# Values three units behind their scores, a fourth tile of transposed exponentials, and 2-D biases loaded by halves

## The chip, the cores and the metric

The kernel runs on one core of a Trainium2 chip. TensorE (PE in the profile) multiplies matrices into eight PSUM banks, VectorE (DVE), ScalarE (ACT) and GpSimd (POOL) work on tiles, and nearly all transfers are issued from SyncE's queue (SP). Each engine takes its instructions in order. The metric is the device time of one execution in microseconds (us); lower is better.

## The reference, cut to what matters

One encoder layer is computed for a prompt of 512 tokens and a sample of 1024 tokens, 1024 wide, with shared weights:

```python
h = rmsnorm(x);  q/k/v of heads A and B, gate logits = split(h @ w_in)
oa = neighborhood_attention(qa, ka, va, rpb)      # 8 heads, 8 x 16 windows on rows of 64 tokens, learned 2-D bias
ob = combine of dilated_group_attention(...)      # 3 groups (dilation 1, 4, 16) x 4 heads, T5 bias,
                                                  # weighted by each group's softmax denominator
x = x + (sigmoid(ga) * (oa @ w_a) + sigmoid(gb) * (ob @ w_b)) @ w_out
x = x + relu(rmsnorm(x) @ w_up)**2 @ w_down
```

All tensors are float32 outside; the kernel computes each product as three float16 matmuls of high and low halves.

## The kernel before, in words

**Stages.** Up to about 157 us the inputs are normalised, the first gate columns are multiplied and bias tables are built in device memory (tb_d, tc_d for B, ba_d for A). Then comes the attention stage, to about 985 us. After it the branch products, the output product and the MLP (dn and up in the profile) run to the end.

**Attention.** Heads are handled in ten pairs, i = 0 to 9: 0 to 5 are B (group g = i mod 3), 6 to 9 are A. ORDER (L39) sets their order, and each is done for the prompt (r = 0) and then for the sample (r = 1). A pair's work is cut into units of 128 queries: four for the prompt, eight for the sample, 120 in all. In the profile's names the first digit is r and the letter the kind: pT1a is the transposed exponentials of a sample A pair.

A unit has two parts. Its scores part (`scores`, L447 to L482) issues four matmuls into two PSUM banks, adds the bias and takes the minimum on VectorE (L462), exponentiates on ScalarE (L464), splits into two float16 halves (ScalarE L478, VectorE L479) in tile p16, and has SP transpose p16 by DMA into a tile of tag pT (L481). Its values part (`values`, L484 to L496) multiplies pT with the values from a tile of tag V (L492, L493), and evicts with ScalarE (L495) and VectorE (L496). An A unit is then normalised on POOL (L537) and stored to o_d by SP (L540); a B unit is stored with its minimum and denominator to g_d (L614).

**Order of the work.** Three generators are advanced in turn, one step each (`run`, L696 to L702). `attention` (L665 to L684) gives out a unit's scores in one step and may give out an older unit's values in the next, so a unit takes two steps. Values are given out when more than `lag` = NPT - 1 units stand in its queue, or when the oldest is AGE steps old; NPT is 3 and AGE 5 (L35, L36). `proj` (L348 to L444) gives in each step half of a 128-token projection (12 matmuls, pj in the profile), squares and normalises q and k, has SP transpose them into tiles qk0 (prompt) or qk1 (sample) (L389), and copies them on ScalarE and VectorE (L394, L395) some tiles later. After the pairs 6, 7 and 8 it gives six gate steps of 24 matmuls (g) each, and at its end the filler `fill`, five gates of three blocks. `combines` (L686 to L694) waits until a pair of group 2 has given out its last unit (`done`), lets eight steps pass, and then loads the three groups' outputs for 256 tokens into a tile G (L626), twice for the prompt and four times for the sample, weights them on VectorE, ScalarE and POOL (L633 to L653) and stores them to o_d (L654).

Within this program order the framework sets each engine's final order at build time, by its own estimate of when an instruction's inputs and buffers are ready.

**Tiles.** Those of one tag share a fixed number of buffers: pT has NPT = 3, V has NV = 5, bias 2, oB (a B unit's output) 4, oA 3, qk0 2, G 2, and mn, den and rd (an A unit's minimum, denominator and its reciprocal) 4 each. A pair's sample bias for A is a tile of 128 x 2 x 768 floats (768 KB, L544, L545) for the columns (0,), (1, 2) and (3,) of j; it serves two or four units. The blocks of x wait in tiles of the attention pool's tags before that stage: block 2's chunks 0 to 5 in two bias tiles (L775 to L777). The row of squared gains (L785) uses a G buffer.

Of the kernel before, what the change touches and what calls it, by code (L numbers as in the profile page):

```python
# [10 lines left out]
F32 = mybir.dt.float32  # L11
# [6 lines left out]
P = 128  # L18
D = 1024
# [12 lines left out]
VEC = 512  # L32
RPW = 63

NPT = 3  # L35
AGE = 5  # L36
NV = 5

ORDER = (0, 1, 2, 6, 3, 7, 4, 8, 5, 9)  # L39
# [91 lines left out]
def encoder(ctx, tc, xt, x, wg, wp, wb, wo, wu, wn, wd, nv, nvr, nmlp, nq, rpb, t5, oneh, negrow, cmask, yp, ys):  # L131
    nc = tc.nc
# [18 lines left out]
    ba_d = [drp.tile([HA, 16, 8, 1024], F32, name=f"ba_d{i}") for i in range(3)]  # L151
# [177 lines left out]
    class Attention:  # L329
# [172 lines left out]
        def attn_a(self, p):  # L502
            for _ in tab:
                pass
            pp, n = self.pp, p["name"]
            h0 = 2 * (p["i"] - 6)

            groups = ((0, 0, 8, 0),) if p["r"] == 0 else ((0, 0, 12, 0), (1, 4, 12, 384))
            c0, cn = (0, 256) if p["r"] == 0 else (256, 768)
            nrb = p["n"] // 256  # L510
            vsrc = self.va(p).rearrange("(r w) b d -> r w b d", w=GW)

            def load_v(j):
                v = self.vtile(f"{n}_{j}")
                nc.sync.dma_start(out=v[:, :nrb], in_=vsrc[:, A_K0[j]:A_K0[j] + 32])
                return v

            def make(j, bias, v, grp):
                blk, r0, nr, b0 = grp
                nm = f"{n}_{j}_{blk}"  # L520
                widths = [P] * (nr // 4)
                st = {}

                def s():
                    mn = pp.tile([P, 2], F32, tag="mn", bufs=4, name=f"mn{nm}")
                    den = pp.tile([P, 2], F32, tag="den", bufs=4, name=f"den{nm}")
                    st["p"] = self.scores(
                        nm, p, lambda q: q[:, (4 * blk + j) * P:(4 * blk + j + 1) * P],
                        lambda k: k.rearrange("p (r c) -> p r c", c=GW)[:, r0:r0 + nr, A_K0[j]:A_K0[j] + 32], widths,
                        [bias[:, h, b0:b0 + nr * 32] for h in range(2)], mn, den)  # L530
                    st["rd"] = pp.tile([P, 2], F32, tag="rd", bufs=4, name=f"rd{nm}")
                    nc.vector.reciprocal(out=st["rd"], in_=den)

                def v_():
                    ot = pp.tile([P, P], F32, tag="oA", bufs=3, name=f"o{nm}")
                    self.values(nm, p, st["p"], widths, [v[:, r0 // 4 + i] for i in range(nr // 4)], ot)
                    nc.gpsimd.tensor_tensor(out=heads(ot), in0=heads(ot), in1=bcast(st["rd"], HD), op=ALU.mult)  # L537
                    a = p["t0"] + blk * 512
                    dst = o_d[a:a + 512].rearrange("(r w) d -> w r d", w=GW)
                    nc.sync.dma_start(out=dst[16 * j:16 * j + 16, :, h0 * HD:h0 * HD + P], in_=ot)  # L540
                return s, v_

            for cg, js in enumerate(((0,), (1, 2), (3,))):
                bias = pp.tile([P, 2, cn], F32, tag="bias", bufs=2, name=f"ba{n}_{cg}")  # L544
                nc.sync.dma_start(out=bias, in_=ba_d[cg][h0:h0 + 2, :, :, c0:c0 + cn].rearrange("h c r k -> (c r) h k"))  # L545
                vt = [load_v(j) for j in js]
                for j, v in zip(js, vt):
                    for grp in groups:
                        yield make(j, bias, v, grp)


        def attn_b(self, p):
            pp, n, g, jj = self.pp, p["name"], p["g"], p["jj"]
            t0, L, nt = p["t0"], p["n"], p["nt"]
            gd = g_d[jj][t0:t0 + L, g]
            vd = v_d[p["i"]][t0:t0 + L]
            tiles = []
            if g < 2:
                bt = pp.tile([P, 2, 384], F32, tag="bias", bufs=2, name=f"b{n}")
                nc.sync.dma_start(out=bt, in_=tb_d[g][2 * jj:2 * jj + 2].rearrange("h p k -> p h k"))  # L560
            else:
                bt = pp.tile([P, 2, P], F32, tag="bias", bufs=2, name=f"b{n}")
                nc.sync.dma_start(out=bt, in_=tc_d[p["r"]][2 * jj:2 * jj + 2].rearrange("h p k -> p h k"))
            if g == 0:
                vts = [self.vtile(f"{n}_{i}") for i in range(-(-(nt + 1) // 4))]

                def chunk(c):
                    return vts[c // 4][:, c % 4, :]
                nc.sync.dma_start(out=chunk(0)[0:64], in_=vd[0:64])
                for i in range(len(vts)):  # L570
                    a, e = max(1, 4 * i), min(nt, 4 * i + 4)
                    if e > a:
                        nc.sync.dma_start(out=vts[i][:, a - 4 * i:e - 4 * i, :],
                                          in_=vd[64 + (a - 1) * P:64 + (e - 1) * P].rearrange("(c p) d -> p c d", p=P))
                nc.sync.dma_start(out=chunk(nt)[0:64], in_=vd[L - 64:L])
                for i in range(nt):
                    w = [64 if i == 0 else P, 64 if i == nt - 1 else P]
                    tiles.append((slice(i * P, (i + 1) * P), slice(max(0, i * P - 64), max(0, i * P - 64) + sum(w)), w,
                                  128 if i == 0 else 64, [chunk(i), chunk(i + 1)],
                                  gd[i * P:(i + 1) * P]))  # L580
            elif g == 1:
                vs = [self.vtile(f"{n}_{i}") for i in range(nt // 4)]
                for i, v in enumerate(vs):
                    nc.sync.dma_start(out=v, in_=vd[i * 512:(i + 1) * 512].rearrange("(i c) d -> i c d", c=4))
                m = nt // 4
                for c in range(4):
                    for i in range(m):
                        a = c + 4 * i * P
                        tiles.append((slice(a, a + 4 * P - 3, 4), slice(c, c + 4 * m * P - 3, 4), [P] * m, 128 - 128 * i,
                                      [v[:, c, :] for v in vs],  # L590
                                      gd.rearrange("(i c) d -> c i d", c=4)[c, i * P:(i + 1) * P]))
            else:

                vs = [self.vtile(f"{n}_{i}") for i in range(nt // 4)]
                for i, v in enumerate(vs):
                    nc.sync.dma_start(out=v, in_=vd.rearrange("(m c) d -> m c d", c=nt)[:, 4 * i:4 * i + 4])
                for t in range(nt):
                    a = slice(t, t + nt * (P - 1) + 1, nt)
                    tiles.append((a, a, [P], 0, [vs[t // 4][:, t % 4, :]], gd.rearrange("(m c) d -> c m d", c=nt)[t]))

            def make(ti):
                qs, ks, widths, boff, vch, dst = tiles[ti]
                nm = f"{n}_{ti}"
                w = sum(widths)
                st = {}

                def s():
                    o = st["o"] = pp.tile([P, 132], F32, tag="oB", bufs=4, name=f"o{nm}")
                    st["p"] = self.scores(nm, p, lambda q: q[:, qs], lambda k: k[:, ks], widths,
                                          [bt[:, h, boff:boff + w] for h in range(2)], o[:, 128:130], o[:, 130:132])  # L610

                def v_():
                    self.values(nm, p, st["p"], widths, vch, st["o"][:, :P])
                    nc.sync.dma_start(out=dst, in_=st["o"])  # L614
                return s, v_

            for ti in range(nt):
                yield make(ti)
            p["done"] = True
# [147 lines left out]
    with tc.tile_pool(name="attention", bufs=1, reuse_waits="tile") as pp:  # L767
        def load_x(b):

            if b < 2:  # L770
                x6 = pp.tile([P, 6, 512], F32, tag="qk1", bufs=2, name=f"xt{b}")
                xch[b] = [x6[:, k] for k in range(6)]
            else:
                xch[b] = []
                for i in range(2):  # L775
                    x3 = pp.tile([P, 3, 512], F32, tag="bias", bufs=2, name=f"xt{b}_{i}")
                    xch[b] += [x3[:, k] for k in range(3)]  # L777
            xch[b] += [pp.tile([P, 512], F32, tag="V", bufs=NV, name=f"xt{b}_{k}") for k in (6, 7)]
            for k, c in enumerate(xch[b]):
                xch["last"] = nc.sync.dma_start(out=c, in_=xt[b, :, k, :]).ins  # L780
                yield

        def gain():

            row = pp.tile([1, D], F32, tag="G", bufs=2, name="nvrow")  # L785
            nc.scalar.dma_start(out=row, in_=nvr)
            nc.vector.tensor_tensor(out=row, in0=row, in1=row, op=ALU.mult)
            mx = pp.tile([1, 2], F32, name="nvmax")
# [497 lines left out]
```

## Time and profile before

| what | before |
|---|---|
| median of 3 runs (lowest, highest) | 2255.98 us (2255.64, 2256.01) |
| the profiled execution, its time | 2257.27 us |
| its span, first to last instruction | 2255.5 us |
| TensorE, matmuls | 2131.3 us busy (94%), x11440 |
| TensorE, weight loads | 1085.5 us (48%) |
| VectorE | 1258.3 us (56%) |
| ScalarE | 1010.4 us (45%) |
| POOL | 314.6 us (14%) |
| mean granted TensorE clock | 0.985 |
| DMA, mean over the span | 111 GB/s |

The busy shares are averages over stages. In the MLP, more than half of the span, TensorE is busy throughout and its wait is for itself; what the change does must be read in the attention stage. A granted clock of 1.00 is 2.4 GHz, 0.5 is 1.2 GHz. "Idle before" an instruction is the time that its engine stood still ahead of it, and the releaser is what ended it.

### The profile page before, as it was taken

Reading aid. Unit: us, or ns where it says so; the run is one execution under the profiler, and the core shown is the slowest. Engines: PE = TensorE matmul, PEld = TensorE weight load, DVE = VectorE, ACT = ScalarE, POOL = GpSimd, SP = SyncE. Lnnn points to the kernel's source line nnn. Section 1 sums busy time; section 2 is a strip of 40 time slices with the busy share of each in tenths; the row PEclk is TensorE's granted clock in tenths of the full one; section 3 lists DMA queues with packets and bytes.
Section 4 is the critical chain, followed back from the end, with each engine's and each line's share of the span. In section 5 each row is a group of like instructions: output and inputs, shape, how many; then the busy total and the mean of one; then the engine's idle time right before and its main releaser. Section 6 shows DMA issues by size and latency. Waiting matters only on the chain.

```text
span 2255.5 us, 32279 instructions
## 1 busy us (share of the span) xinstructions
PE 2131.3 (94%) x11440; PEld 1085.5 (48%) x11440; DVE 1258.3 (56%) x3231; ACT 1010.4 (45%) x2435; POOL 314.6 (14%) x445
## 2 busy tenths in 40 slices
PE   5898899899989989899999999999999999999999
PEld 3355555455555555344444544444444444444444
DVE  7646767676577577556644644444444444444444
ACT  6346765477566566346622532222333333323222
POOL 5123332242232232100000000000000000000000
PEclk9899999999999999899999999999999999999999
DMA  6676656877776776877530111101111111110102
GB/s 202 203 237 144 140 133 143 171 167 163 160 165 132 158 153 135 191 238 237 159 108 29 57 56 49 35 30 57 57 57 56 56 57 56 56 37 24 34 1 112
DMA packets 342187, 251.23 MB, mean 111 GB/s; under 512 B 210432, under 2 KB 302464, under 8 KB 342024
## 3 DMA queue, kind: packets, MB, share of 16 engines
q1 hardware_dynamic: 341878, 249.15, 42.3%
q8 instruction: 90, 1.47, 0.3%
q14 instruction: 73, 0.60, 0.1%
q10 hardware_dynamic: 146, 0.01, 0.0%
HBM read 164.02 MB, written 53.29 MB: 96 GB/s over the span
## 4 chain that ended last, share of the span: by engine, by line
PE 54%; DMA 1%; issue 1%; ACT 0%; DVE 0%; SPq 0%; POOL 0%; ACTq 0%; DVEq 0%; POOLq 0%
PE up L174 7%; PE dn L174 7%; PE dn L176 7%; PE up L176 7%; PE up L175 7%; PE dn L175 7%; PE op L174 2%; PE op L176 2%; PE op L175 2%; PE br L174 1%; PE br L175 1%; PE br L176 1%; DMA z<-z_d 0%; DMA st_b<-in_wb 0%; PE hT L1041 0%
## 5 line engine op out<-in xcount | busy, mean ns | idle before, releaser
L943 DVE SCALAR_TENSOR_TENSOR y<-dn,und,y 128x512 f32<-128x512 f32 x384 | 287.1, 750 | 179.4 <-PE dn L176 178.8
L1121 ACT ACTIVATE r<-up,alpha 128x512 f32<-128x512 f32 x96 | 65.3, 681 | 592.1 <-PE up L176 592.0
L174 PE MATMUL up<-xp,w_u 128*128 128x512 f16 x768 | 291.0, 379 | 1.0 <-ACT xp L1044 1.0
L176 PE MATMUL dn<-w_d,u 128*128 128x512 f16 x768 | 291.1, 379 | 0.0
L176 PE MATMUL up<-xp,w_u 128*128 128x512 f16 x768 | 291.0, 379 | 0.0
L175 PE MATMUL dn<-w_d,u 128*128 128x512 f16 x768 | 291.0, 379 | 0.0
L175 PE MATMUL up<-xp,w_u 128*128 128x512 f16 x768 | 291.0, 379 | 0.0
L174 PE MATMUL dn<-w_d,u 128*128 128x512 f16 x768 | 291.0, 379 | 0.0
L1125 DVE TENSOR_TENSOR u<-r,u 128x512 f16<-128x512 f32 x96 | 66.4, 692 | 284.5 <-ACT u L1124 280.7
L174 PE MATMUL g<-act,w_g 128*128 128x512 f16 x384 | 148.6, 391 | 23.6 <-ACT act L802 13.7
L175 PE MATMUL g<-act,w_g 128*128 128x512 f16 x384 | 149.3, 389 | 7.4 <-DVE act L803 7.4
L176 PE MATMUL g<-act,w_g 128*128 128x512 f16 x384 | 149.4, 389 | 1.2 <-DVE w_g L263 1.0
L174 PE MATMUL pj1b<-w_p,act 128*128 128x384 f16 x384 | 126.1, 328 | 5.6 <-DVE qn0b L380 3.6
L175 PEld LDWEIGHTS <-act 128*128 128x128 f16 x960 | 96.2, 100 | 68.0 <-issue 15.6
L176 PEld LDWEIGHTS <-act 128*128 128x128 f16 x960 | 95.6, 100 | 65.7 <-issue 5.7
L174 PEld LDWEIGHTS <-act 128*128 128x128 f16 x960 | 96.8, 101 | 62.5 <-issue 4.8
L176 PE MATMUL pj1b<-w_p,act 128*128 128x384 f16 x384 | 125.9, 328 | 0.0
L175 PE MATMUL pj1b<-w_p,act 128*128 128x384 f16 x384 | 125.8, 328 | 0.0
L174 PEld LDWEIGHTS <-u 128*128 128x128 f16 x768 | 76.3, 99 | 88.9
L174 PEld LDWEIGHTS <-w_u 128*128 128x128 f16 x768 | 76.4, 100 | 88.5
L176 PEld LDWEIGHTS <-u 128*128 128x128 f16 x768 | 75.1, 98 | 90.7
L176 PEld LDWEIGHTS <-w_u 128*128 128x128 f16 x768 | 75.1, 98 | 90.5
(331 smaller groups left out, 4260.1 us busy)
## 6 DMA issues: line engine op xcount, KB each, us to landing
st_n<-in_wn SPq DMA_DIRECT2D x32, 512.0 KB
st_u<-in_wu SPq DMA_DIRECT2D x32, 512.0 KB
st_d<-in_wd SPq DMA_DIRECT2D x32, 512.0 KB
st_p<-in_wp SPq DMA_DIRECT2D x80, 192.0 KB
z_d<-z SPq DMA_DIRECT2D x48, 256.0 KB
z<-z_d SPq DMA_DIRECT2D x48, 256.0 KB
ba1a<-ba_d SPq DMA_DIRECT2D x12, 768.0 KB
xt<-in_xt SPq DMA_DIRECT2D x24, 256.0 KB
```

The source lines that it names most:

```text
L174: nc.tensor.matmul(ps, ah, bh, start=first, stop=False)
L175: nc.tensor.matmul(ps, ah, bl, start=False, stop=False)
L176: nc.tensor.matmul(ps, al, bh, start=False, stop=last)
L943: nc.vector.scalar_tensor_tensor(out=out, in0=ps, scalar=scale, in1=out, op0=ALU.mult, op1=ALU.add)
L1121: nc.scalar.activation(s, ps[b], AF.Relu, scale=alpha[:, f:f + 1])
L1125: nc.vector.tensor_tensor(out=uu[:, 1, i, tb], in0=s, in1=uu[:, 0, i, tb], op=ALU.subtract)
```

## The change

Values follow their scores by three units instead of two (lag = NPT - 1), or after 7 steps instead of 5, and there are four pT and five oB buffers. A's bias for the sample is loaded in two tiles of 384 columns, one for each block of 512 tokens, into three bias buffers; the units of columns 1 and 2 then run by block first (j 1, 2 of block 0, then of block 1). Block 2 of x uses one qk0 tile for three chunks and three bias tiles for three, and the gains' row uses a qk0 buffer.

```diff
-NPT = 3
-AGE = 5
+NPT = 4
+AGE = 7
...
-            groups = ((0, 0, 8, 0),) if p["r"] == 0 else ((0, 0, 12, 0), (1, 4, 12, 384))
-            c0, cn = (0, 256) if p["r"] == 0 else (256, 768)
+            groups = ((0, 0, 8, 0),) if p["r"] == 0 else ((0, 0, 12, 256), (1, 4, 12, 640))
...
-                        [bias[:, h, b0:b0 + nr * 32] for h in range(2)], mn, den)
+                        [bias[:, h] for h in range(2)], mn, den)
...
             for cg, js in enumerate(((0,), (1, 2), (3,))):
-                bias = pp.tile([P, 2, cn], F32, tag="bias", bufs=2, name=f"ba{n}_{cg}")
-                nc.sync.dma_start(out=bias, in_=ba_d[cg][h0:h0 + 2, :, :, c0:c0 + cn].rearrange("h c r k -> (c r) h k"))
-                vt = [load_v(j) for j in js]
-                for j, v in zip(js, vt):
-                    for grp in groups:
+                vt = None
+                for grp in groups:
+                    c0, cn = grp[3], grp[2] * 32
+                    bias = pp.tile([P, 2, cn], F32, tag="bias", bufs=3, name=f"ba{n}_{cg}_{grp[0]}")
+                    nc.sync.dma_start(out=bias, in_=ba_d[cg][h0:h0 + 2, :, :, c0:c0 + cn].rearrange("h c r k -> (c r) h k"))
+                    vt = vt or [load_v(j) for j in js]
+                    for j, v in zip(js, vt):
                         yield make(j, bias, v, grp)
...
-                    o = st["o"] = pp.tile([P, 132], F32, tag="oB", bufs=4, name=f"o{nm}")
+                    o = st["o"] = pp.tile([P, 132], F32, tag="oB", bufs=5, name=f"o{nm}")
...
-                for i in range(2):
-                    x3 = pp.tile([P, 3, 512], F32, tag="bias", bufs=2, name=f"xt{b}_{i}")
-                    xch[b] += [x3[:, k] for k in range(3)]
+                x3 = pp.tile([P, 3, 512], F32, tag="qk0", bufs=2, name=f"xt{b}")
+                xch[b] += [x3[:, k] for k in range(3)]
+                xch[b] += [pp.tile([P, 512], F32, tag="bias", bufs=3, name=f"xt{b}_{k}") for k in range(3, 6)]
...
-            row = pp.tile([1, D], F32, tag="G", bufs=2, name="nvrow")
+            row = pp.tile([1, D], F32, tag="qk0", bufs=2, name="nvrow")
```

The bias tiles of the B pairs also change from two buffers to three, with no other difference.

## Rows read from the trace of the kernel before

**Rows 1.** Stretches: us, PE, PEld, DVE, ACT, POOL busy (instructions), clock, DMA, GB/s.

```profile
265.00:306.00 41.00, 41.00 (x285) 25.27 (x284) 29.66 (x104) 26.76 (x82) 12.74 (x17) 1.00 0.50 112
...
430.00:479.00 49.00, 43.03 (x307) 26.12 (x305) 40.41 (x156) 34.53 (x98) 19.18 (x26) 0.97 0.73 157
...
600.00:649.00 49.00, 42.27 (x301) 25.78 (x299) 37.78 (x124) 37.70 (x106) 16.28 (x24) 0.97 0.78 163
...
767.00:814.00 47.00, 41.54 (x307) 25.63 (x305) 35.79 (x120) 34.41 (x98) 15.90 (x24) 1.00 0.68 146
...
907.00:947.00 40.00, 30.02 (x144) 13.21 (x141) 20.94 (x96) 12.60 (x34) 3.87 (x9) 0.83 0.90 200
```

**Rows 2.** Waits of TensorE: waiter, waited for, us in total, times, longest.

```profile
PE o1a L492 <- DMA pT1a<-p1a: 20.5, 13, 3.9
...
PE o1b L492 <- DMA pT1b<-p1b: 6.6, 6, 1.8
PE g L174 <- ACT z L184: 5.0, 1, 5.0
...
PE g L174 <- DVE z L186: 4.5, 1, 4.5
...
PE o0a L492 <- DMA pT0a<-p0a: 2.9, 4, 1.4
...
PE o0b L492 <- DMA pT0b<-p0b: 2.4, 1, 2.4
```

**Rows 3.** Timeline of one unit: start, us, engine, line, names (TensorE, VectorE, SP).

```profile
629.58 0.49 PE L460 MATMUL s1a<-qk1a,qa1a 128*128 128x384 f16 x2
...
637.91 0.96 DVE L479 SCALAR_TENSOR_TENSOR p1a<-s21a,p1a 128x768 f16<-128x768 f32 x1 [0.58 <-ACT p1a L478]
...
639.04 1.62 SPq L481 DMA_TRANSPOSE pT1a<-p1a  x1
...
645.09 0.29 PE L492 MATMUL o1a<-v1a,pT1a 128*128 128x128 f16 x1 [2.14 <-DMA pT1a<-p1a]
```

**Rows 4.** Waits of VectorE: waiter, waited for, us in total, times, longest.

```profile
DVE qk1b L395 <- DMA qk1b<-q161b: 41.9, 29, 3.5
DVE qk0b L395 <- DMA qk0b<-q160b: 35.9, 19, 6.6
...
DVE cm L633 <- DMA G<-g_d: 24.9, 8, 11.0
```

**Rows 5.** Stretches behind three waits, same columns as Rows 1.

```profile
488.00:492.00 4.00, 4.00 (x17) 2.04 (x16) 2.78 (x13) 2.96 (x12) 2.26 (x3) 0.57 0.85 192
...
645.00:649.00 4.00, 3.91 (x23) 2.44 (x24) 3.31 (x9) 3.45 (x10) 0.85 (x2) 0.57 0.58 180
...
662.00:666.00 4.00, 4.00 (x21) 2.14 (x19) 2.56 (x12) 2.52 (x9) 1.90 (x3) 0.57 0.64 100
```

**Rows 6.** Timeline of TensorE in the first pair.

```profile
184.68 0.29 PE L492 MATMUL o0b<-v0b,pT0b 128*128 128x128 f16 x1 [3.29 <-ACT o0b L495]
```

**Rows 7.** Timeline of the last two values, and the gate matmuls (PE, DVE, ACT).

```profile
978.37 0.22 PE L492 MATMUL o1a<-v1a,pT1a 128*128 128x128 f16 x1
...
984.05 0.22 PE L492 MATMUL o1a<-v1a,pT1a 128*128 128x128 f16 x1
...
876.80:985.00 108.20, 85.67 (x361) 5.21 (x7) 5.40 (x8) 0.94 0.71 164
```

**Rows 8.** The tile ba1a: its issues (ns min/median/max), and its list of waiters.

```profile
L545 SPq DMA_DIRECT2D ba1a<-ba_d x12: 359/376/931, 408.3 to 935.1; - x12
...
who waited for it (us, times):
busy tenths in 40 slices 0000000010010010100000000000000000000000
```

**Rows 9.** The tiles xt and qk0b: last read of x, first transpose into qk0.

```profile
L803 DVE SCALAR_TENSOR_TENSOR act<-xt,nvt,act x24: 736/744/1816, 28.3 to 105.7; 128x512 f16<-128x512 f32 x24
...
L389 SPq DMA_TRANSPOSE qk0b<-q160b x24: 1190/1244/1968, 137.3 to 781.4; - x24
```

**Rows 10.** Waits of SP's queue for the stores that G reads.

```profile
SPq L626 <- DMA g_d<-o1b: 9.7, 2, 5.2
```

More of the change, by code (lines that the diff above doesn't have):

```diff
@@ L518, in make @@
             def make(j, bias, v, grp):
-                blk, r0, nr, b0 = grp
+                blk, r0, nr, _ = grp
                 nm = f"{n}_{j}_{blk}"
@@ L558, in attn_b @@
             if g < 2:
-                bt = pp.tile([P, 2, 384], F32, tag="bias", bufs=2, name=f"b{n}")
+                bt = pp.tile([P, 2, 384], F32, tag="bias", bufs=3, name=f"b{n}")
                 nc.sync.dma_start(out=bt, in_=tb_d[g][2 * jj:2 * jj + 2].rearrange("h p k -> p h k"))
             else:
-                bt = pp.tile([P, 2, P], F32, tag="bias", bufs=2, name=f"b{n}")
+                bt = pp.tile([P, 2, P], F32, tag="bias", bufs=3, name=f"b{n}")
                 nc.sync.dma_start(out=bt, in_=tc_d[p["r"]][2 * jj:2 * jj + 2].rearrange("h p k -> p h k"))
```

## The prediction

> **What bounds the kernel now.** I read the busy time by stage first, then TensorE's waits, then one unit in order of time, then VectorE's waits.
>
> The change touches the attention stage, 157 to 985 us of the span. Its eight-unit stretches tell where TensorE is short of time [rows 1]. From 265 to 306 us (a 1024-token B pair) it is busy 41.0 of 41.0 us: eight units take 41.0 us, 5.1 us each, and nothing holds it up. In the three shown of the four stretches with 1024-token A pairs it is busy 43.0 of 49, 42.3 of 49 and 41.5 of 47 us, so 18.2 us are lost. The reader should see that VectorE (40.4, 37.8, 35.8 us) is busy too, though less.
>
> TensorE's waits say what it is short of [rows 2]. Its value matmuls (L492) wait for the transposed exponentials pT: 20.5, 6.6, 2.9 and 2.4 us, together 32.4 us in 24 waits, the longest 3.9 us. No other cause in the attention stage is as large; the two gate waits of 5.0 and 4.5 us in the same rows come back under the rivals.
>
> One unit shows the chain [rows 3]. Its scores start at 629.58; VectorE writes the last half of its exponentials (L479) at 637.91; SP issues the transpose at 639.04; the value matmul starts at 645.09 after 2.14 us of waiting. So 15.5 us passed from scores to values, three units' time, and that was not quite enough. TensorE works in order, so projections and gates stand behind each such wait.
>
> VectorE has waits of its own in the same stage: for the transposes of q and k, 41.9 and 35.9 us in the two largest groups, and 24.9 us for the group outputs G of the combination [rows 4]. They do not move with the change.
>
> **The change part by part.** The sum is made against the profiled execution, 2257.3 us (span 2255.5), which is 1.3 us over the median of the runs, 2256.0.
>
> *Values one unit later (lag 3, AGE 7, a fourth pT).* Each of the 120 units keeps all its instructions. What moves two steps (one unit) later is its values part: 4 to 12 matmuls, the ACT and DVE eviction (L495, L496), for A the POOL normalisation, and the store on SP. The transpose's place does not move, so the time that it has grows by one unit, 5.1 us by rows 1. The longest of the 24 waits is 3.9 us, so all would go if nothing else got later. For the B pairs and the prompt's A pairs I take that in full: 6.6 + 2.9 + 2.4 = 11.9 us. For the 1024-token A pairs I take half of 20.5, 10.3 us: in 600 to 649 us VectorE is busy 37.8 us; without the pT waits of such a stretch (about 5 us, a quarter of 20.5) it would last 44, VectorE would be busy 86% of it, and with its waits for q and k some of its lateness reaches TensorE through score banks that are not free. The ends are 0 and 20.5.
>
> *Clock.* Three pT waits end at half clock: in the 4 us after 488, 645 and 662 us the mean granted clock is 0.57 [rows 5], each after a stretch with TensorE waiting, so 0.43 x 4 = 1.7 us each, 5.2 together. I take half with the A pairs' waits, 2.6; ends 0 and 5.2.
>
> *The first pair.* At 184.68 a value matmul waits 3.29 us, by the profile for ScalarE's eviction [rows 6]; with AGE 7 it comes two steps later. I take 0; ends 0 and 3.3.
>
> *Tiles that now turn over later.* The transpose of unit n+4 needs the tile that V(n) frees; V(n) stands one step behind S(n+3), as V(n) stood one step behind S(n+2) with three tiles: no new wait. rd keeps four buffers and is now used fully: its fifth user writes about 8 us after its scores (629.58 to 637.91 in rows 3 bounds it), V(n) starts half a unit ahead of those scores: free in time. V tiles (NV stays 5) are held one unit longer, so a load of values can start 5.1 us later, but its first reader also comes a unit later. I take 0; the upper end is one unit, 5.1 us, at each of the two 1024-token pairs of group 0, which with the prompt's tiles use all five: 10.2.
>
> *The tail.* The last values are drained by age, now 7 steps after their scores. The gate matmuls that cover the drain number 361 up to 985 us, that is 15 gate steps of 24 and the first of the next [rows 7]: all the filler there is (5 gates, 3 blocks). So the last two V's will stand side by side ahead of gate 15's 72 matmuls, where a gate step lay between them (978.37 and 984.05). Cost 0.6 us, one V's matmuls; if the drain slips by a whole gate step instead, 5.7 us, the distance of those two rows.
>
> *Biases by halves.* 12 loads of 768 KB become 24 of 384 KB, the same bytes: 12 more issues at 0.38 us median [rows 8], 4.5 us of SP's time over 530 us. Nobody waited for this tile (its list of waiters is empty), and with three half tiles the next half is asked for at least three units before its scores, 15 us. Nothing on the path; ends 0 and 4.5 if SP delayed a transpose each time, which the extra unit covers. What this part buys is room: 3 KB less bias, 3 KB more pT.
>
> *x and gain rows in other tiles.* The same loads. Block 2's last read of x ends before 108 us; the first q/k transpose into qk0 is at 137.3 [rows 9]. 0.
>
> The Trainium skill (Perfetto Trace Analysis, Identifying the Most-Contended Engine) says that matmul busy time is a poor measure of TensorE, that weight-load busy time is a better one, and that the engine with the highest occupancy should be improved first. By that rule the 600 to 649 us stretch, weight loads 25.8 of 49 us against 37.8 for VectorE, belongs to VectorE, and the 20.5 us of the A pairs are not to be had: the sum would be the first rival's. The rows agree with it on which engine is busier by that measure; that TensorE, busy 42.3 us by its matmuls, stands still for the rest is what speaks against it.
>
> **Sum.** 11.9 + 10.3 + 2.6 - 0.6 = 24.2; 2257.3 - 24.2 = 2233.1, less 1.3 is 2232 for the median. With all upper ends, 32.4 + 5.2 + 3.3 - 0.6 = 40.3, it is 2216; with nothing from the A pairs and the clock, 11.3, it is 2245.
>
> **The rivals.**
>
> *VectorE takes over (0.20).* TensorE arrives earlier at the next score matmuls and waits there for banks that VectorE has not read. For it: VectorE's busy time in the A stretches and its 41.9 and 35.9 us of waiting for q and k [rows 4], which also hold ScalarE's exponentials back. Against it: it is still idle 11 us of 49. Then only the 11.9 us remain at best, 2245, and half of them at worst, 2251 with some loss in the tail up to 2256.
>
> *The combination blocks the queues (0.16), the slower side.* G is loaded a fixed 8 steps after a group's last unit was given out; that unit's values, which write what G reads, now come 5 steps after that point instead of 3. SP waits in order for that write: 9.7 us in two waits already [rows 10], and VectorE behind it up to 11.0 us at once [rows 4]. What one such block costs is seen from 907 to 947 us: TensorE busy 30.0 of 40 us at a mean clock of 0.83 [rows 1], 10.0 + 0.17 x 40 = 16.8 us. Four pair ends have such a load; two block today, and the point that decides is whether at the other two the write lands after SP has reached the load. If both do, 33.6 us are lost against 24.2 gained: 2256 + 9.4 = 2265, from 2258 to 2275 with the gain's ends. Against it: the write also moves up in SP's order ahead of G, and with the biases by halves less is queued in front of it.
>
> *It does not do what it says (0.04).* The order of each engine's instructions is chosen at build time from estimated readiness; V may already have been placed late enough in that order that one unit of lag hardly moves it. Then 2253 to 2258.
>
> **How the numbers follow.** The forecast case has 0.60, its own range 2216 to 2245. 0.2% is 4.5 us, about what can be told from no change. Faster by more (under 2251.5): 0.60 and 0.12 of VectorE's 0.20, 0.72. Within: its other 0.08 and the last rival's 0.04, 0.12. Slower: 0.16. The range 2216 to 2257 leaves out the slower case and little else.
>
> **What would show it.** Right: the L492 waits for pT fall from 32.4 us to under 10 and the span loses most of that; the A stretches shorten from 49 to some 45 us; the half clock behind 488, 645 and 662 us is gone. VectorE's rival: the pT waits vanish, but waits of L174 and L460 for DVE's L380 and L462 grow by as much. The combination's rival: more and longer waits of SP's L626 for g_d, and new stretches like 907 to 947. The forecast fails if pT waits stay over 15 us, or if the attention stage still ends at 985 us.

## The result, and the profile after

The change makes the kernel slower: 2269.87 us median of five runs (2262.68 to 2277.03) against 2255.98 us, a ratio of 1.0061 (95% interval 1.0043 to 1.0079). The forecast was 2232 us, the range 2216 to 2257.

The page of the changed kernel (time 2270.31 us), its span and busy times:

```profile
span 2268.4 us, 32284 instructions
...
PE 2135.3 (94%) x11440; PEld 1086.5 (48%) x11440; DVE 1260.1 (56%) x3231; ACT 1011.3 (45%) x2435; POOL 315.9 (14%) x445
```

The span grew by 12.9 us (2255.5 to 2268.4). TensorE's 11440 matmuls took 4.0 us longer in sum (2131.3 to 2135.3); the other 8.9 us are idle time. The stretch from the first score matmul to the first branch matmul tells where (the MLP, which the text on the kernel before puts at more than half of the span, takes 1008 of its 2255.5 us, from 1247.9 us on, and is not touched). Stretches of the kernel before, then of the changed kernel (columns as in Rows 1):

```profile
157.30:1004.70 847.40, 773.99 (x5035) 450.05 (x5033) 564.71 (x2064) 500.08 (x1541) 227.11 (x330) 0.97 0.70 155
```

```profile
156.20:1016.80 860.60, 776.99 (x5035) 451.07 (x5033) 567.25 (x2065) 501.82 (x1543) 228.69 (x330) 0.97 0.69 153
657.00:661.00 4.00, 3.34 (x12) 1.68 (x12) 4.00 (x11) 3.69 (x14) 0.85 (x2) 0.64 0.51 151
```

All of it is there: the stage is 13.2 us longer, 10.2 us of that TensorE's idle time (73.4 to 83.6) and 3.0 us longer matmuls. Half clock did not go, it moved: the granted clock falls to half in ten stretches of the stage before and in eleven after, one of them behind 657 us.

Cut at the first score matmul of each pair, the loss stands in the six 1024-token B pairs. The sums over their stretches (us, then busy time by engine), in the kernel before and in the changed one:

```profile
sum 279.53, PE 265.49 PEld 157.67 DVE 208.35 ACT 177.63 POOL 85.95; mean PE 44.25 PEld 26.28 DVE 34.73 ACT 29.60 POOL 14.32
```

```profile
sum 297.69, PE 267.03 PEld 157.09 DVE 214.10 ACT 182.03 POOL 91.51; mean PE 44.50 PEld 26.18 DVE 35.68 ACT 30.34 POOL 15.25
```

They are 18.2 us longer, and TensorE's idle time in them goes from 14.0 to 30.7 us. The four 1024-token A pairs, which were to give 10.3 us of the gain, took 203.3 us before and 204.9 after (the last counted to its last scores): the first 48.2 and 55.4 (the prompt pair ahead of it got 6.2 shorter), the second and third 49.1 and 46.2 before, 45.5 and 45.4 after. The 512-token A pairs took 166.7 and 158.2, the 512-token B pairs 159.9 and 161.6.

TensorE's waits from 140 to 1010 us in the changed kernel (columns as in Rows 2):

```profile
PE t0b L460 <- DVE o1a L496: 7.7, 3, 3.5
...
PE t1a L460 <- DVE mn1a L462: 6.2, 2, 6.0
PE pj1a L174 <- DVE qn0a L380: 5.3, 5, 1.2
PE pj1a L174 <- DVE qn1a L380: 4.9, 7, 1.2
PE t1b L460 <- DVE qn1a L380: 4.7, 3, 2.2
...
PE o0b L492 <- DMA pT0b<-p0b: 4.0, 1, 4.0
PE t1b L460 <- DVE o1b L496: 3.6, 5, 1.7
...
PE o1a L492 <- DMA pT1a<-p1a: 1.5, 1, 1.5
```

The waits for pT are nearly gone: 4.0 and 1.5 us are left of 32.4 us. In their place stand the score matmuls (L460) and the first matmul of a projection or gate (L174), which wait for VectorE to read a PSUM bank. Summed over all rows of this view, L460 and L174 waited 19.8 us for VectorE before and 65.0 after. In the 1024-token B pairs alone these went from 8.9 to 28.0 us, where the waits for pT had been only 2.1 us; in the 1024-token A pairs from 8.1 to 23.1, where 11.5 us of waits for pT went in exchange. The values matmuls (L492) had waited 11.0 us for VectorE and now wait 1.2. Taken over the stage's own bounds, as in the stretches above, all waits together come to 73.0 us before and 83.0 after, so they hold 10.0 of the 10.2 us of added idle time.

One of the new waits in order of time. TensorE, then VectorE (start, us, line, names, and in brackets the idle time before it and what ended it):

```profile
653.80 0.40 PE L460 MATMUL s0b<-qk0b 128*128 128x128 f16 x2
...
657.66 0.39 PE L460 MATMUL t0b<-qk0b 128*128 128x128 f16 x2 [3.46 <-DVE o1a L496]
```

```profile
654.04 0.62 DVE L263 SCALAR_TENSOR_TENSOR w_g<-st_g,scales,w_g 128x384 f16<-128x384 f32 x1 [0.20 <-ACT w_g L262]
656.61 0.22 DVE L395 COPY qk1b<-qk1b 64x256 f16<-64x256 f16 x1 [1.94 <-DMA qk1b<-q161b]
656.86 0.48 DVE L263 SCALAR_TENSOR_TENSOR w_g<-st_g,scales,w_g 128x256 f16<-128x256 f32 x1
657.26 0.35 DVE L496 SCALAR_TENSOR_TENSOR o1a<-o1a,unscale_v,o1a 128x128 f32<-128x128 f32 x1
657.52 0.41 DVE L380 TENSOR_TENSOR qn1b<-pj1b,rq1b 128x256 f32<-128x256 f32 x1
657.86 0.61 DVE L462 CUSTOM_DVE_ANT_0 s21a<-s1a,ba1a,unscale 128x384 f32<-128x384 f32 x1
```

Read it backwards. The second head's score matmul starts at 657.66, when the eviction of an older unit (L496, 657.26) has given its bank free. VectorE came to that eviction late: 1.94 of the 3.46 us it stood at L395, the copy of q and k, whose transpose had not landed. A projection (L380) and the scores of the unit before (L462, 657.86) were queued behind it too. The same picture stands at 824.67 (3.53 us, of which VectorE stood 2.85 us at L395). All PSUM tiles share one tag of eight buffers (L135, L138), and a unit's two steps take four of them: two for scores, one for values, one for a projection. So by this count TensorE can be about two units ahead of VectorE and ScalarE, and no further.

SP's waits for the stores that G reads, and three of VectorE's waits, in the changed kernel:

```profile
SPq L627 <- DMA g_d<-o1b: 9.3, 2, 5.1
```

```profile
DVE qk1b L395 <- DMA qk1b<-q161b: 35.3, 33, 3.8
DVE cm L634 <- DMA G<-g_d: 33.1, 11, 7.6
DVE qk0b L395 <- DMA qk0b<-q160b: 32.1, 18, 5.4
```

The combination's waits are no larger on SP (9.7 us in [rows 10]), and VectorE's longest block there is shorter (7.6 against 11.0 in [rows 4]), though in sum VectorE waited 33.1 us for G against 24.9. Nor did the tail cost much: the first branch matmul came 37.8 us behind the last score matmul before (966.84) and 38.2 us behind it after (978.58), with the last two values side by side (from 995.79 and 996.53). From the first to the last of the gate matmuls that end the stage, among which the last pair's units run, it took 107.0 us before (877.8 on) and 106.0 after (891.1 on); the stage was already 13.3 us late when it got there.

### The profile page after: what moved, and what is told of

Read it like the earlier page. It is cut to its first block, busy times and chain, and to the rows that moved or that the text cites. A ratio compares the mean times of both kernels' runs of the same rounds, so it can differ in the third digit from the quotient of the medians.

```text
span 2268.4 us, 32284 instructions
## 1 busy us (share of the span) xinstructions
PE 2135.3 (94%) x11440; PEld 1086.5 (48%) x11440; DVE 1260.1 (56%) x3231; ACT 1011.3 (45%) x2435; POOL 315.9 (14%) x445
## 3 DMA queue, kind: packets, MB, share of 16 engines
q1 hardware_dynamic: 345142, 249.15, 42.1%
## 4 chain that ended last, share of the span: by engine, by line
PE 63%; DMA 17%; DVE 9%; ACT 6%; issue 3%; POOL 1%; SPq 1%; POOLq 0%; ACTq 0%; DVEq 0%
PE up L174 7%; PE dn L174 7%; PE dn L175 7%; PE up L175 7%; PE up L176 7%; PE dn L176 7%; DMA qk1b<-q161b 4%; DMA qk0b<-q160b 3%; PE g L175 2%; PE g L174 2%; PE g L176 2%; DMA qk1a<-q161a 2%; PE op L176 2%; PE op L174 2%; PE op L175 2%
## 5 line engine op out<-in xcount | busy, mean ns | idle before, releaser
L174 PE MATMUL up<-xp,w_u 128*128 128x512 f16 x768 | 291.0, 379 | 1.0 <-ACT xp L1045 1.0
L174 PE MATMUL dn<-w_d,u 128*128 128x512 f16 x768 | 291.0, 379 | 0.0
L174 PE MATMUL g<-act,w_g 128*128 128x512 f16 x384 | 148.0, 390 | 18.0 <-ACT z L184 6.2
L174 PE MATMUL pj1b<-w_p,act 128*128 128x384 f16 x384 | 128.2, 334 | 14.8 <-DVE scales L195 4.5
L175 PEld LDWEIGHTS <-act 128*128 128x128 f16 x960 | 95.8, 100 | 89.8 <-issue 38.8
L176 PE MATMUL pj1b<-w_p,act 128*128 128x384 f16 x384 | 128.1, 334 | 0.0
L175 PE MATMUL pj1b<-w_p,act 128*128 128x384 f16 x384 | 127.8, 333 | 0.0
L174 PEld LDWEIGHTS <-act 128*128 128x128 f16 x960 | 96.6, 101 | 61.5 <-issue 6.7
L174 PEld LDWEIGHTS <-u 128*128 128x128 f16 x768 | 76.3, 99 | 89.0
L174 PEld LDWEIGHTS <-w_u 128*128 128x128 f16 x768 | 76.4, 100 | 88.5
```

The source lines that it names most:

```text
L174: nc.tensor.matmul(ps, ah, bh, start=first, stop=False)
L175: nc.tensor.matmul(ps, ah, bl, start=False, stop=False)
L176: nc.tensor.matmul(ps, al, bh, start=False, stop=last)
```

## The experiments

Each ratio is to the kernel before on the same chip in the same job. The theory: the longer lag costs what it saves, and more, because TensorE now runs into banks that VectorE has not read, and VectorE is late because it stands at the copy of L395 (124.6 us in all before; ScalarE stands 146.6 us at its own, L394). Rivals: the halved bias loads cost; or the banks do it alone, whatever VectorE's standing. No run moves the copies of one of the two engines alone, so what is said below of VectorE's standing holds for that of both together.

### e1 and e2: which part of the change costs

e1 is the changed kernel with the old lag (three pT), e2 the kernel before with the new lag alone:

```diff
-NPT = 4
-AGE = 7
+NPT = 3
+AGE = 5
```

```diff
-NPT = 3
-AGE = 5
+NPT = 4
+AGE = 7
...
-                    o = st["o"] = pp.tile([P, 132], F32, tag="oB", bufs=4, name=f"o{nm}")
+                    o = st["o"] = pp.tile([P, 132], F32, tag="oB", bufs=5, name=f"o{nm}")
...
-            row = pp.tile([1, D], F32, tag="G", bufs=2, name="nvrow")
+            row = pp.tile([1, D], F32, tag="qk0", bufs=2, name="nvrow")
```

> Biases by halves and the moved x and gain tiles alone; three pT, lag 2, AGE 5 as before. Queue theory (the values' lag only changes which TensorE instruction stands behind VectorE, and what it costs extra comes from the lag): within 4 us of before, 2252 to 2260, pT waits still 25 to 40 us. Bias theory (twice the issues on SP delay the transposes): 2264 to 2272, and SP's waits or the transposes' lateness grow.

> Lag 3, AGE 7, four pT, five oB, with the 2-D biases in whole tiles as before. Queue theory: slower than before by 7 to 20 us, 2263 to 2276, pT waits under 8 us and waits of L460 and L174 for VectorE grown by 30 us or more. Bias theory: faster than before by 10 us or more, under 2246.

e1: 2259.93 against 2259.12 us, 1.0004 (0.9992 to 1.0015), with 35.3 us of waits for pT. e2: 2270.15 us, 1.0052 (1.0036 to 1.0068). The loads by halves cost nothing that can be told; the longer lag carries the loss. In e2 the waits for pT are 7.5 us, and L460 and L174 wait 66.9 us for VectorE. The bias tile of the changed kernel, its loads and its list of waiters:

```profile
L547 SPq DMA_DIRECT2D ba1a<-ba_d x24: 370/470/801, 390.7 to 960.6; - x24
its engine sat idle before it (us, times) until:
who waited for it (us, times):
```

### e3 and e4: the copies given out later

To shorten VectorE's standing, the copies of q and k are given out one projection tile later in the program, in the kernel before (e3) and the changed one (e4):

```diff
-            late, later, last = [], [], []
+            late, later, last, oldest = [], [], [], []
...
-                            for l in last:
+                            for l in oldest:
                                 arrange(*l)
-                            later, last = [], later
+                            oldest, last, later = last, later, []
```

> The kernel before, with the copies of q and k (arrange) given out one projection tile (3.9 us) later. Queue theory: VectorE's waits at L395 fall from 124.6 us in all to under 60, ScalarE's at L394 likewise, the pT waits of TensorE fall from 32.4 to under 20, and the time falls by 8 us or more, to 2248 or less. If TensorE's own chain of scores, transposes and values sets the time, nothing changes but the start of each pair, 2254 to 2262.

> The changed kernel with the same later arrange. Queue theory: the bank waits of TensorE (L460 and L174 for VectorE, some 75 us of gaps with the others) fall by 25 us or more and the time falls below before, 2235 to 2250. Bias theory and combination theory (G blocks the queues): stays at 2264 to 2274.

Neither gained: e3 2270.77 us, 1.0049 (1.0034 to 1.0064), slower than either of its bands; e4 2273.62 us, 1.0065 (1.0046 to 1.0084), in the band of its two rivals (the bias, which e1 and e2 speak against, and the combination) and where the changed kernel stood. VectorE still waited 119.5 us at L395 in e3, against 124.6 in the kernel before, and 122.1 in e4. So a later place in the program did not move the copies behind their transposes; and a pair is ready later (e3's first scores start at 162.4 us instead of 157.3). As it left the standing as it was, this edit could not tell the theories apart.

### e5 and e6: fewer banks for a unit

The scores of both heads go into one buffer where they fit (up to 256 columns each), so that such a unit takes three of the eight (a sample A unit, with 384 columns a head, still four): e5 in the changed kernel, e6 in the kernel before.

```diff
-            pss = [psum(f"s{nm}"), psum(f"t{nm}")]
+            if n <= 256:
+                ps1 = psum(f"s{nm}")
+                pss = [ps1[:, 0:256], ps1[:, 256:512]]
+            else:
+                pss = [psum(f"s{nm}"), psum(f"t{nm}")]
```

> The changed kernel, with both heads' scores in one PSUM bank where a unit has at most 256 keys (all B units and the prompt's A units, 88 of 120). Bank theory (with lag 3 TensorE stops at score and projection matmuls whose bank VectorE has not read): the gaps of L174 and L460 behind VectorE, 65 us in the changed kernel, fall by 20 us or more, and the time by 10 us or more, to 2260 or less. If the changed kernel is held by the queues themselves and not by the number of banks: within 5 us of it, 2265 to 2275.

> The kernel before, with the same sharing of banks. Bank theory: it stops at pT (32 us) and only 20 us at banks, so it gains little, 2250 to 2260, and less than the changed kernel gains. If banks hold both alike: it gains as much as the changed kernel, 2245 or less.

e5: 2253.17 against 2254.41 us, 0.9990 (0.9980 to 1.0001): the whole loss is gone, with VectorE still standing 117.2 us at the copies. e6: 2256.07 us, 1.0008 (0.9997 to 1.0018): the same edit gives nothing with the short lag, where TensorE then waits 63.8 us for pT. In e5 L460's waits for VectorE (L464 there) fell from 30.8 to 6.1 us. And the gain falls where the edit acts. The 1024-token B pairs in e5:

```profile
sum 271.16, PE 260.76 PEld 156.20 DVE 197.05 ACT 165.88 POOL 83.56; mean PE 43.46 PEld 26.03 DVE 32.84 ACT 27.65 POOL 13.93
```

They take 271.2 us instead of 297.7, and L464 and L174 wait 3.3 us for VectorE there instead of 28.0. The 1024-token A pairs, whose units still take two buffers for their scores, do not gain: 210.3 against 204.9 us, and 24.9 us of such waits against 23.1. At the pair end that was read above, TensorE (e5):

```profile
639.72 0.53 PE L464 MATMUL s0b<-qk0b 128*128 128x128 f16 x3
...
643.11 0.48 PE L174 MATMUL pj0a<-w_p,act 128*128 128x384 f16 x1 [2.86 <-DVE o1a L500]
```

The scores now go through, and the projection behind them is caught by the same late eviction, for 2.86 us: the lead is longer, not endless.

### e7 and e8: no waiting for q and k

The copies (L394, L395, L399) read a tile of zeros, in the kernel before (e7) and the changed one (e8); the copied parts of q and k are thus left out of the attention. Every instruction stays.

```diff
+    czero = wp_.tile([P, 2, P], F16, name="czero")
...
-                nc.vector.tensor_copy(p["qk"][:h, 4:6, ts], p["qk"][h:, 2:4, ts])
+                nc.vector.tensor_copy(p["qk"][:h, 4:6, ts], czero[h:])
```

> The kernel before, in which the copies of q and k (L394, L395, L399) read a tile of zeros instead of the transposed q and k, so that ScalarE and VectorE never wait there for SP's transposes; the attention is computed from these. Queue theory (VectorE and ScalarE standing at these copies make both the exponentials and the evictions late): their 124.6 and 146.6 us of waits go, TensorE's pT waits fall under 15 us and the time falls by 15 us or more, to 2241 or less. If TensorE's waits come from the transposes' own time: within 5 us of before.

> The changed kernel with the same zeros in the copies. Queue theory: bank gaps fall from 65 us to under 35, the time falls by 25 us or more from 2270, to 2245 or less, and with VectorE free the lag of three no longer loses: within 5 us of the run without waits on the kernel before, or faster. If the lag of three costs by itself (more values open at once): it stays 8 us or more above that run.

e7: 2224.90 us, 0.9865 (0.9849 to 0.9881). e8: 2224.19 us, 0.9864 (0.9848 to 0.9879). The standing of both engines at the copies costs the kernel before about 30 us, and without it the longer lag neither loses nor gains. One part of e7's expectation failed: the waits for pT, which were to fall under 15 us, are still 27.3. They stand in the 512-token pairs (26.1 us); in the 1024-token pairs they are gone (13.6 to 1.4 us), and TensorE's idle time there goes from 42.1 to 15.2 us. (The first scores come at 172.1 us in e7 and 170.1 in e8, against 157.3, so their stages compare with each other and not with the others.) The longer lag still trades one wait for another: the waits for pT go from 27.3 to 3.5 us, those of scores, projections and gates for VectorE from 10.0 to 32.3.

### e9 to e12: the copies behind ready work

An order edge puts each copy behind the newest split of q and k given out (L386, L387) in its engine's queue, so that the engine does that work first while the transpose lands:

```diff
-                nc.scalar.activation(q16[:, 0:8:2], heads(qn), AF.Copy, scale=QSCALE)
+                fin[0] = nc.scalar.activation(q16[:, 0:8:2], heads(qn), AF.Copy, scale=QSCALE).ins
...
+                with tc.issue_after(fin[0]):
+                    nc.scalar.activation(p["qk"][h:, 4:6, ts], p["qk"][:h, 2:4, ts], AF.Copy)
+                with tc.issue_after(fin[1]):
+                    nc.vector.tensor_copy(p["qk"][:h, 4:6, ts], p["qk"][h:, 2:4, ts])
```

e9 is the kernel before with this, e10 with e6's shared buffer too, e11 the changed kernel with both, e12 the changed kernel with the order alone.

> The kernel before, in which each of the copies L394 and L395 must stand in its engine's order behind the newest q/k split (L386, L387) that has been given out, so behind the next tile's instead of its own; every result is computed as before. Queue theory: the waits at L395 fall from 124.6 us to under 70 and the time falls by 8 to 20 us, 2235 to 2247. If the order on VectorE does not matter, because the transposes are late against any place: within 5 us of before.

> Lag 2, the shared score bank and the later place of the copies. Queue theory: like the run with the order alone or a few us better, 2232 to 2247, with pT waits of 10 to 30 us left.

> The changed kernel with the shared score bank and the later place of the copies. Queue and bank theory: faster than before by 10 to 25 us, 2230 to 2245, and not slower than the same with lag 2. If the lag of three costs by itself: 5 us or more above the lag 2 run.

> The changed kernel with the copies of L394/L395 put behind the newest split given out (as in e9), and two banks for a unit's scores as it has. If what the lag of three lost came from VectorE standing at those copies, so that evictions and exponentials were late at the banks, the loss goes with the standing: within 3 us of the 2234.8 us that the kernel before came to with the same order. If the banks of the third unit cost something by themselves, 7 to 15 us more than that (2242 to 2250 us), with the sum of TensorE's waits for VectorE at L460 and at the projection's matmul still over 30 us between 140 and 1010 us.

e9: 2234.79 us, 0.9906 (0.9889 to 0.9923). e10: 2235.71 us, 0.9921 (0.9900 to 0.9943). e11: 2231.97 us, 0.9893 (0.9878 to 0.9909). e12: 2246.30 us, 0.9977 (0.9967 to 0.9986). The order halves VectorE's standing for q and k (124.6 us before; in e9 23.1 at L397, the copy, and 34.1 at L401, the next one for A; in e12 25.3 and 39.6) and takes more of ScalarE's (146.6 us at L394 before, 29.9 at L395 in e9), and both lags gain by it. In e10 the waits for pT are 45.5 us and not the 10 to 30 expected. But e12 lands in the second band of its expectation: with the order the longer lag still loses, and its sum at L460 and L174 is 42.2 us, over the 30 named. So with half of VectorE's standing the banks still cost, and the shared buffer is again what takes that away (e12 to e11); only with none of it (e8) is the exchange even.

The attention stage of e9, e12 and e11, one fence each (columns as in Rows 1):

```profile
154.80:982.30 827.50, 769.80 (x5035) 451.29 (x5033) 571.96 (x2064) 500.56 (x1541) 229.99 (x330) 0.97 0.73 159
```

```profile
159.20:993.70 834.50, 772.52 (x5034) 450.20 (x5033) 569.45 (x2061) 500.05 (x1539) 225.94 (x330) 0.98 0.70 158
```

```profile
158.30:979.50 821.20, 764.31 (x5033) 448.66 (x5032) 570.34 (x2061) 499.49 (x1539) 226.62 (x330) 0.98 0.73 159
```

e12's stage is 7.0 us longer than e9's, and it begins 4.4 us later, for a reason that these runs do not tell. TensorE's waits from 140 to 1010 us, e9 and then e12 (scores are at L462 in both, values at L494):

```profile
PE o1a L494 <- DMA pT1a<-p1a: 18.1, 12, 4.2
PE o0a L494 <- DMA pT0a<-p0a: 6.7, 4, 3.7
...
PE o0b L494 <- DMA pT0b<-p0b: 4.7, 1, 4.7
PE o1b L494 <- DMA pT1b<-p1b: 3.9, 4, 2.0
```

```profile
...
PE pj1a L174 <- DVE qn1a L380: 4.9, 2, 3.3
PE pj1a L174 <- DVE o1b L464: 4.1, 2, 3.3
PE pj1b L174 <- DVE o0a L498: 3.8, 1, 3.8
PE o0b L494 <- DMA pT0b<-p0b: 3.6, 1, 3.6
PE t1b L462 <- DVE o1b L498: 3.5, 3, 1.6
...
PE o1a L494 <- DMA pT1a<-p1a: 2.0, 2, 1.1
```

The reader should see the exchange: in e9 the top rows are values waiting for pT, in e12, below one gate row, scores and projections waiting for VectorE's reads (L380, L464, L498). All pairs side by side; the stage is that of one profiled execution, and the waits are sums over the rows of each list, us:

| edit | ratio, lag 2 and lag 3 | stage, lag 2 and lag 3 | its 1024-token B pairs | waits for pT | scores, projections, gates for VectorE |
|---|---|---|---|---|---|
| none | 1, 1.0061 | 847.4, 860.6 | 279.5, 297.7 | 32.4, 5.5 | 19.8, 65.0 |
| order (e9, e12) | 0.9906, 0.9977 | 827.5, 834.5 | 270.5, 289.4 | 33.4, 5.6 | 14.4, 42.2 |
| no waiting (e7, e8) | 0.9865, 0.9864 | 803.2, 802.4 | 259.5, 266.2 | 27.3, 3.5 | 10.0, 32.3 |
| shared buffer (e6, e5) | 1.0008, 0.9990 | 852.6, 841.7 | 276.6, 271.2 | 63.8, 9.5 | 9.6, 38.8 |
| both (e10, e11) | 0.9921, 0.9893 | 826.8, 821.2 | 269.7, 270.3 | 45.5, 16.2 | 6.4, 19.3 |

Down the first three pairs VectorE and ScalarE stand less and less at the copies, and the longer lag costs the stage 13.2, 7.0 and then less than nothing (in the 1024-token B pairs 18.2, 18.9 and 6.7). In the last two a unit takes fewer buffers, and the longer lag shortens the stage by 10.9 and 5.6 us (in time 2256.07 to 2253.17 and 2235.71 to 2231.97 us, where the runs of each two overlap). e11 beats the kernel before by 24 us, the changed one by about 38; its interval overlaps e9's, which needs neither the lag nor the shared buffer.

## Why the prediction was wrong

*The waits for pT.* Right in place and size: under 10 us were forecast, 5.5 are left, and the tiles that turn over later (pT, rd, V) made no wait that the lists show: SP's transposes waited 40.6 us for TensorE against 47.5, and no wait of TensorE is for rd or V.

*The step that failed* is to take the waits for pT as gained: 10.3 us of them for the 1024-token A pairs and 11.9 us "in full" for the rest. The prediction said that "some of its lateness reaches TensorE through score banks that are not free", but only for the 1024-token A pairs, and sized it at half of one row. Over the stage it came to 65.0 - 19.8 = 45.2 us of new waits for VectorE at L460 and L174, and 4.8 of smaller ones, more than the 26.9 us of pT and the 13.1 us of the values matmuls' waits for VectorE and ScalarE that went. The 1024-token A pairs got 1.6 us longer in place of 10.3 shorter (the second and third came to the 45 us forecast, the first did not), and the 1024-token B pairs, where the prediction saw no price at all, 18.2 us longer. What should have been asked: with the pT wait gone, how far can TensorE run before the next thing stops it? The answer was countable beforehand, eight buffers over four a unit, two units. That the pT waits had kept TensorE within that fits the runs and was not measured by itself. The prediction counted pT, V, rd and bias buffers, and not PSUM.

*VectorE takes over (0.20).* The right mechanism, with the very lines named ("waits of L174 and L460 for DVE's L380 and L462"), but bounded at 2256 because it was only allowed to eat the gain. Nothing in it excluded a loss: late work on VectorE delays the scores and the evictions alike, and every stop of TensorE can bring a stretch at half clock behind it.

*VectorE's waits for q and k.* The prediction read them [rows 4] and set them aside: "They do not move with the change." They moved little (124.6 to 114.6 us; ScalarE's at L394 146.6 to 159.8), but they decided what the change was worth: e7 against before says 30 us, e8 against e7 that without them the loss is gone. The prediction weighed the Trainium skill's rule (Perfetto Trace Analysis, Identifying the Most-Contended Engine) that the engine with the highest occupancy comes first; the runs agree in part: the edits at VectorE's and ScalarE's queues (e7, e9) gained most, but they do not part the two. What e7 and e9 add is that it was not busy time that counted (VectorE 1258.3 us before, 1252.1 in e7, 1264.5 in e9), but where the engines stood still.

The Trainium skill also says that the same gap repeating on an engine that should be saturated can mean too little PSUM for the next tile (Perfetto Trace Analysis, Optimization Strategy). e5 agrees: one buffer less a unit, 0.9990 where the changed kernel has 1.0061, some 16 us.

*Clock.* A gain of 2.6 us was forecast; the stage's matmuls took 3.0 us longer instead, and half clock stands behind new waits (657 and 825 us) as it had behind old ones.

*First pair, tail, biases by halves, combination.* Right in the main. The wait in the first pair stayed in another form (4.0 us for pT0b), the tail cost 0.4 us (0.6 forecast), the halves cost 1.0004 (0.9992 to 1.0015), and the combination's rival did not come about as told: SP's waits are the same. VectorE's waits for G did grow by 8.2 us, at the loads from 419 to 446 us (13.1 us against 5.0), where the first 1024-token A pair got longer and the prompt pair ahead of it shorter; what this is worth no run tells, but e5 has 30.7 us of the same waits and none of the loss. The result lies in the time of that rival, slower, 2258 to 2275 us, by luck: the reason was another.

*What stays open.* How much of the standing's price is VectorE's and how much ScalarE's. Why the exchange is a loss and not even in the full kernel is shown only by the pairs (the loss shrinks with the standing, and goes with the shared buffer where that acts), not traced wait by wait.

## What to carry to other kernels

When a wait on the critical engine is taken away, count what stops the engine next: how many buffers of its scarcest pool one unit of work takes, and how far behind the readers of that pool are. A wait that looks like pure loss may be what keeps an engine inside its buffers. And look at what an engine stands for at the head of its queue: work that is ready behind one early-placed instruction is late for everyone, and moving such an instruction on two engines (e9) was worth 21 us, where the longer lag cost 14.

## What the runs showed of the hardware

A standstill of TensorE was often followed by half clock: nine of the eleven stretches at half clock in the changed kernel begin within 3 us of the end of a wait of 1.5 us or more, or during it; nine other waits as long had none. In the changed kernel a score matmul waited 5.97 us until 454.90; what VectorE did first, and two stretches (columns as in Rows 1):

```profile
452.52 0.22 DVE L395 COPY qk0b<-qk0b 64x256 f16<-64x256 f16 x1 [2.29 <-DMA qk0b<-q160b]
```

```profile
454.00:460.00 6.00, 5.10 (x22) 2.45 (x22) 6.00 (x23) 4.53 (x14) 3.98 (x6) 0.50 0.38 83
460.00:465.00 5.00, 5.00 (x39) 3.25 (x37) 4.17 (x22) 2.66 (x8) 2.63 (x5) 0.99 0.94 165
```

The granted clock is 0.50 (1.2 GHz) from 454 to 460 us, and 0.99 in the next five. VectorE had stood 2.29 us at L395, and was busy 6.00 of those 6 us: work had piled up behind one late transfer (small operations of the combination among it) and was then done without a break, while TensorE ran at half speed.
